# A two-layer trunk on one core: attention scores on 128 partitions, and two late FFNs that begin with plain pairs

## The chip, the cores and the metric

The kernel runs on one core of one Trainium2 chip. The metric is the device time of one execution in microseconds. Three runs of the kernel before took 2305.58, 2306.04 and 2314.34 us; the median is 2306.04 us.

## The reference

The input has 512 positions of 1024 features, in float32. Two layers, each with two half-step SwiGLU FFNs of 2816 hidden units, a mixer between them (retention in layer 0, forgetting attention in layer 1), and a gated per-layer embedding at the end. Every step is preceded by an RMS norm, and a last norm ends the trunk.

```python
for i in range(DEPTH):
    h = h + 0.5 * swiglu(rmsnorm(h, nw[0]), ffn_w_in[i, 0], ffn_w_out[i, 0])
    hn = rmsnorm(h, nw[1])
    h = h + (retention(hn, ...) if i % 2 == 0 else forgetting_attention(hn, ...))
    h = h + 0.5 * swiglu(rmsnorm(h, nw[2]), ffn_w_in[i, 1], ffn_w_out[i, 1])
    gate = sigmoid(rmsnorm(h, nw[3]) @ ple_w_gate[i])
    h = h + gate * (p[i] @ ple_w_proj[i])
return rmsnorm(h, final_norm_w)

# forgetting attention: 16 heads of 64, causal
log_f = log_sigmoid(fz + b_f)          # one gate per position and head
c = cumsum(log_f)
logits = q @ k.T * DH ** -0.5 + c[query] - c[key]
o = softmax(logits) @ v
```

## The kernel before, in words

**Numbers.** A float32 value is split into a high part that TensorE takes as it is and a low part, the rest. A product of two split values is three matmuls, high by high, high by low, low by high (`mm3`, L300 to L303). `split` (L289) makes the parts of an activation: ScalarE copies the high part, VectorE subtracts it (lines L292 and L293). Weights are loaded through `wraw` buffers, cast on ScalarE (L79), and their low part is made on VectorE or GpSimd (L80). Activations lie with features on partitions: eight blocks of 128 features by 512 positions, `h[0]` to `h[7]`.

**Norms.** The gain goes into the split; the factor per position is applied at the end of a step. `columns` (L421) adds up the squares with eight tiny matmuls (L426), and VectorE makes the reciprocal root from them (`cols`, L448 to L454). `rows` (L436) turns the result with four transposes (L445) and copies it to `rows` on ScalarE, as the factor for every product of this norm.

**FFN.** A pair is the two products, gate and up, for 128 hidden units. Most pairs take a scheme of seven instead of eight half-size products: `one` (L517), `two` (L522) and `three` (L533), all through `product` (L475, matmuls at L478), 84 matmuls of 256 columns. They need sums of weight quarters (`emit_sums`, L131) and sums of activation quarters, which `Norm.quarters` (L354) makes from each finished block of `h` on ScalarE and VectorE under names such as `t1` and `b21`. `plain` (L496) is a pair by eight products, 96 matmuls of 256 columns, with no sums. The first FFN begins with two plain pairs; the other three begin with `one` of pairs 0 and 1. Pairs are worked off in three chunks, each followed by its eight output blocks (`out_blocks`, L560).

**Retention** (L679) begins with the q and k products of head 0, then columns and rows, then v (`v_part`, L662). Its output products of the last two heads share banks (`out_both`, L634).

**Forgetting attention** (L824) has eight pairs of heads, each with its k product (`k_part`, L889), its q product (`q_part`, L906) and scores (L923). For k the low part lies in one tile `klo`, 64 partitions per head, so the matmul at L933 contracts over 64 partitions. The one at L936 contracts over 128: high and low part of q on the one side, the high part of k twice on the other. VectorE then does the softmax from the scores' banks (L955 to L967), with the gates' sums from `cdram`. `turn` (L972) transposes the probabilities, ten transposes per head at L982, into three banks, which ScalarE and VectorE split into `thi` and `tlo`. `attend` (L988) multiplies them by v (L995, L996) and adds the halves (L998 on ScalarE, L999 on VectorE). `out_part` (L620) does the output in two halves of heads, each added to `h` on its own. The gates' chain runs over 16 partitions from L836 to L868, on VectorE for the most part.

**What sets the order.** TensorE's order is the order in which the code is written. For the other engines a scheduler decides. Weights come in the order of `W.plan` (L215 to L253), two ahead of use. Eight PSUM banks rotate through one pool (`bank`, L277); a bank comes free when the last engine has read it. Which pool of activation buffers a norm takes is set at L1149 (`ua` and `ud` with 16 buffers, `ub`, `uc`).

## Time and profile before

| | |
|---|---|
| runs, median | 2306.04 us (2305.58 to 2314.34) |
| profiled execution, its own time | 2314.51 us |
| span of its profile | 2312.6 us |
| PE busy | 2192.7 us, 95% of the span, 13417 matmuls |
| DVE busy | 1537.3 us, 66% |
| ACT busy | 1210.0 us, 52% |
| POOL busy | 460.0 us, 20% |
| mean granted TensorE clock | 0.966 |

PE is TensorE's matmuls, DVE is VectorE, ACT is ScalarE, POOL is GpSimd. The profiled execution took 2314.51 us, 1.9 more than its span and 8.5 more than the median of the runs. Matmuls overlap one another, so TensorE's busy time is no measure of how densely they run: for that the starts of successive matmuls are compared. The granted clock is given as a share of full speed, 2.4 GHz; its lower level is 1.2 GHz.

### The profile page before, as it was taken

Reading aid. Unit: us, or ns where it says so; the run is one execution under the profiler, and the core shown is the slowest. Engines: PE = TensorE matmul, PEld = TensorE weight load, DVE = VectorE, ACT = ScalarE, POOL = GpSimd, SP = SyncE. Lnnn points to the kernel's source line nnn. Section 1 sums busy time; section 2 is a strip of 40 time slices with the busy share of each in tenths; the row PEclk is TensorE's granted clock in tenths of the full one; section 3 lists DMA queues with packets and bytes.
Section 4 is the critical chain, followed back from the end, with each engine's and each line's share of the span. In section 5 each row is a group of like instructions: output and inputs, shape, how many; then the busy total and the mean of one; then the engine's idle time right before and its main releaser. Section 6 shows DMA issues by size and latency. Waiting matters only on the chain.

```text
span 2312.6 us, 34447 instructions
## 1 busy us (share of the span) xinstructions
PE 2192.7 (95%) x13417; PEld 1955.9 (85%) x13417; DVE 1537.3 (66%) x2813; ACT 1210.0 (52%) x2022; POOL 460.0 (20%) x347
## 2 busy tenths in 40 slices
PE   7998999999999899999989899999999989999998
PEld 7898987888888798989879899897777779898977
DVE  8676766264453976767687676776775787676774
ACT  7464554333233673646466455455564576363653
POOL 0010103344443010101101011014222211010144
PEclk9999999999999999999999999999889989999998
DMA  6474652222322464646345465543222246464631
GB/s 192 119 179 123 150 143 93 75 96 73 100 82 73 119 163 129 156 131 157 105 127 121 130 150 152 145 115 101 65 64 82 69 108 163 117 160 132 147 109 37
DMA packets 87907, 274.94 MB, mean 119 GB/s; under 512 B 9648, under 2 KB 13232, under 8 KB 87744
## 3 DMA queue, kind: packets, MB, share of 16 engines
q1 hardware_dynamic: 63328, 209.78, 27.7%
q0 software_dynamic: 23184, 61.88, 16.0%
q8 instruction: 105, 1.72, 0.3%
q10 hardware_dynamic: 1232, 1.09, 0.1%
q14 instruction: 58, 0.48, 0.1%
HBM read 270.58 MB, written 2.13 MB: 118 GB/s over the span
## 4 chain that ended last, share of the span: by engine, by line
PE 73%; DVE 10%; ACT 7%; DMA 6%; issue 2%; POOL 0%; SPq 0%; ACTq 0%; DVEq 0%; POOLq 0%
PE bank L478 24%; PE bank L303 13%; PE bank L301 13%; PE bank L302 13%; DMA wraw<-in_ffn_w_in 5%; DVE sums L141 2%; PE bank L673 2%; PE bank L674 2%; PE bank L675 2%; ACT w L117 1%; ACT s L79 1%; DVE w L80 1%; ACT w L118 1%; PE bank L936 1%; PE bank L933 1%
## 5 line engine op out<-in xcount | busy, mean ns | idle before, releaser
L79 ACT CAST w<-wraw 128x1024 fp32r<-128x1024 f32 (+1 forms) x224 | 226.7, 1020 | 443.3 <-PE bank L303 286.4
L80 DVE TENSOR_TENSOR s<-sums,s 128x512 fp32r<-128x512 f32 x344 | 232.6, 687 | 116.0 <-ACT s L79 115.5
L79 ACT CAST s<-sums 128x512 fp32r<-128x512 f32 x344 | 208.2, 617 | 190.4 <-DVE sums L141 139.1
L303 PE MATMUL bank<-unit_a,w 128*128 128x512 f32 (+1 forms) x752 | 292.3, 389 | 4.4 <-DVE w L80 2.7
L301 PE MATMUL bank<-unit_a,w 128*128 128x512 f32 (+1 forms) x752 | 293.4, 390 | 2.4 <-ACT w L79 2.0
L302 PE MATMUL bank<-unit_a,w 128*128 128x512 f32 (+1 forms) x752 | 291.8, 388 | 0.8 <-DVE unit_a L293 0.8
L301 PE MATMUL bank<-unit_d,w 128*128 128x512 f32 (+1 forms) x744 | 287.4, 386 | 3.6 <-ACT w L79 1.8
L302 PE MATMUL bank<-unit_d,w 128*128 128x512 f32 (+1 forms) x744 | 285.6, 384 | 5.1 <-DVE unit_d L296 3.9
L303 PE MATMUL bank<-unit_d,w 128*128 128x512 f32 (+1 forms) x744 | 285.0, 383 | 2.7 <-DVE w L80 2.7
L80 POOL TENSOR_TENSOR w<-wraw,w 128x1024 fp32r<-128x1024 f32 x90 | 220.1, 2449 | 323.5 <-ACT w L79 312.5
L478 PE MATMUL bank<-unit_b,s 128*128 128x256 f32 x952 | 205.1, 282 | 0.0
L119 POOL DMA_DIRECT2D a<-in_ffn_w_in x86 | 75.2, 874 | 612.2 <-ACT a L118 540.3
L478 PE MATMUL bank<-unit_d,s 128*128 128x256 f32 x1188 | 194.3, 281 | 0.0
L119 POOL DMA_DIRECT2D w<-in_ffn_w_in x75 | 65.6, 875 | 645.2 <-ACT w L118 518.2
L478 PE MATMUL bank<-unit_a,s 128*128 128x256 f32 x1314 | 186.6, 279 | 2.9 <-ACT unit_a L361 2.4
L302 PEld LDWEIGHTS bank<-unit_d,w 128*128 128x128 f32 x744 | 145.1, 195 | 32.2 <-DVE unit_d L296 4.1
L141 DVE TENSOR_TENSOR sums<-wraw 128x512 f32<-128x512 f32 x172 | 118.0, 688 | 81.6 <-DMA wraw<-in_ffn_w_in 80.3
L301 PEld LDWEIGHTS bank<-unit_d,w 128*128 128x128 f32 x744 | 145.3, 195 | 31.5 <-ACT w L79 3.5
L478 PE MATMUL bank<-unit_b,w 128*128 128x256 f32 x774 | 147.7, 291 | 25.2 <-ACT tmp L529 24.6
L303 PEld LDWEIGHTS bank<-unit_a,w 128*128 128x128 f32 x752 | 141.5, 188 | 35.5 <-DVE w L80 4.5
L569 DVE SCALAR_TENSOR_TENSOR tmp<-bank,rows 128x512 f32<-128x512 f32 x96 | 66.0, 689 | 158.2 <-PE bank L303 154.5
L478 PEld LDWEIGHTS bank<-unit_a,s 128*128 128x128 f32 x1314 | 167.7, 190 | 3.5 <-ACT unit_a L361 2.6
(266 smaller groups left out, 4942.9 us busy)
## 6 DMA issues: line engine op xcount, KB each, us to landing
wraw<-in_ffn_w_in SPq DMA_DIRECT2D x174, 512.0 KB, 4.6
w<-in_ffn_w_in POOLq DMA_DIRECT2D x75, 512.0 KB, 5.6
wraw<-in_ffn_w_out SPq DMA_DIRECT2D x64, 512.0 KB, 5.0
a<-in_ffn_w_in POOLq DMA_DIRECT2D x86, 256.0 KB, 6.5
wraw<-in_ffn_w_out SPq DMA_DIRECT2D x32, 384.0 KB, 4.3
wraw<-in_ret_qk SPq DMA_DIRECT2D x16, 512.0 KB, 3.4
wraw<-in_ret_v SPq DMA_DIRECT2D x16, 512.0 KB, 3.7
wraw<-in_ret_g SPq DMA_DIRECT2D x16, 512.0 KB, 3.5
```

Of the source, the lines that this page charges most:

```text
L79: self.nc.scalar.copy(hi, raw)
L80: self.low.tensor_tensor(out=lo, in0=raw, in1=hi.bitcast(F32), op=ALU.subtract)
L119: self.nc.gpsimd.dma_start(out=lo, in_=src, accum_op=ALU.add)
L141: add = lambda o, p, q: nc.vector.tensor_tensor(out=o, in0=p, in1=q, op=ALU.add)
L301: nc.tensor.matmul(out, wh, xh, start=first, stop=False)
L302: nc.tensor.matmul(out, wh, xl, start=False, stop=False)
L303: nc.tensor.matmul(out, wl, xh, start=False, stop=last)
L478: add = lambda w, x, start, stop: nc.tensor.matmul(out, w, x, start=start, stop=stop, skip_group_check=True)
L569: nc.vector.scalar_tensor_tensor(out=t1, in0=o, scalar=-0.5, in1=n.r, op0=ALU.mult, op1=ALU.mult)
L673: nc.tensor.matmul(os[t], xh, wh[:, js], start=k == 0, stop=False)
L674: nc.tensor.matmul(os[t], xh, wl[:, js], start=False, stop=False)
L675: nc.tensor.matmul(os[t], xl, wh[:, js], start=False, stop=k == KB - 1)
```

## The change

Five pieces.

1. The third and fourth FFN also begin with two plain pairs, in the order low half of positions first; the columns come between the two, the rows behind `one` of the third pair. `quarters` makes `b21` earlier, and a new form `b12` for the even blocks with the last block of a norm; four more buffers of `ua` hold it (`extra`).
2. In the first FFN columns and rows move behind further products.
3. In retention the rows of the norm move behind v.
4. In the attention the k product of pair 0 goes ahead of the columns, its q product ahead of the rows. The low parts of k lie in two tiles of 128 partitions, the other half of each set to zero, so all score matmuls contract over 128 partitions. In a pair the order is now: k, q, attend 0, attend 1, turn 0, turn 1, scores.
5. In the attention's output the two halves of heads add up in the same bank (`OutBoth`), with six banks held open for the first half, and one addition to `h` per block instead of two.

```diff
-CHUNKS = ((0, 8), (8, 16), (16, 22))
-CHUNKS0 = ((0, 6), (6, 14), (14, 22))
+PLAIN = (2, 0, 2, 2)
+CHUNKS = [((0, 6), (6, 14), (14, 22)) if n else ((0, 8), (8, 16), (16, 22)) for n in PLAIN]
...
@@ Norm.quarters
+                if "b21" not in form:
+                    oh, ol = self.unit(), self.unit()
+                    part(o, oh, ol, slice(0, S))
+                    form.update(b21=(oh[:, c0], ol[:, c0]), b22=(oh[:, c1], ol[:, c1]))
+                if b == KB - 1 and self.extra:
+                    for j, x in enumerate(self.forms):
+                        u = unit(self.extra)
+                        x["b12"] = u[:, c0], u[:, c1]
+                        split(h[2 * j][:, c1], *x["b12"], self.gain[:, 2 * j : 2 * j + 1])
...
@@ plain
+            order = [(k, t) for k in range(KB) for t in range(2)]
+            if i:
+                order.sort(key=lambda kt: kt[1])
+            for k, t in order:
...
@@ ffn
-        if i == 0:
-            whole = [plain(m) for m in range(PLAIN)]
-            begun = done = PLAIN
-            n.columns()
-            start(begun)
-            one(begun)
+        if PLAIN[i]:
+            done = PLAIN[i]
+            whole = [plain(m) for m in range(done - 1)]
+            if i:
+                n.columns()
+            whole.append(plain(done - 1))
+            start(done)
+            one(done)
+            if not i:
+                n.columns()
+                two(done)
+                start(done + 1)
+                one(done + 1)
             n.rows()
             for m, (g, u) in enumerate(whole):
                 gated(m, g, u, True)
-            two(begun)
-            begun += 1
+            two(done + 1 if not i else done)
+            begun = done + (1 if i else 2)
...
@@ OutBoth
+        def first(self, ms):
+            for m in ms:
+                self.banks[m] = bank()
+                self.add(0, m)
+
+        def rest(self):
+            for m in range(KB):
+                if m not in self.banks:
+                    self.first([m])
+                self.add(1, m)
+                nc.vector.tensor_tensor(out=h[m], in0=self.banks[m], in1=h[m], op=ALU.add)
+                self.nxt.block(m)
...
@@ retention
-                    n.rows()
-                    nc.scalar.mul(epsv, spread(n.v), EPS)
...
                 vs = v_part(ret_v[hd], n)
+                if hd == 0:
+                    n.rows()
+                    nc.scalar.mul(epsv, spread(n.v), EPS)
...
@@ forgetting
             (fz,) = proj([a["fox_f"]], n)
+            begun = [proj([s], n)[0] for s in fox_qk[0][0:1]]
             n.columns()
+            begun += proj(fox_qk[0][1:2], n)
             n.rows()
...
+            lows = []
+            for e in range(2):
+                lows.append(pool.tile([P, S], F32R, name=f"klo{e}"))
+                nc.gpsimd.memset(lows[e].bitcast(F32), 0.0)
...
-                            nc.tensor.matmul(at[i], q[e][own[e], i * P : w], klo[own[e], :w], start=True, stop=False)
+                            nc.tensor.matmul(at[i], q[e][:, i * P : w], lows[e][:, :w], start=True, stop=False)
...
+            both = OutBoth([(fox_o[0], yhi, ylo), (fox_o[1], [], [])], nxt)
             for p in range(8):
+                if p < 7:
+                    k, q = k_part(p + 1), q_part(p + 1)
                 else:
+                    both.first((0, 1))
                 if old:
                     y = temp()
+                    for e in range(2):
+                        attend(p - 1, e, v, old[e], y)
                     split_y(y)
                 if p == 4:
                     v = v_block(1)
+                if p == 7:
+                    both.first((2, 3))
+                old = [turn(e, sm[e]) for e in range(2)]
+                if p < 7:
                     sm = scores(p + 1, q, k)
+            both.first((4, 5))
...
-    where = (wide_ad, ((ua, 16),), wide_ad, ((ua, 16),), wide_dd, ((ud, 16),), wide_dd, ((ud, 16),))
+    bca, bcd, bdc = ((ub, 8), (uc, 4), (ua, 16)), ((ub, 8), (uc, 4), (ud, 16)), ((ub, 8), (ud, 16), (uc, 4))
+    where = (bca, ((ua, 16),), bca, ((ua, 16),), bdc, ((ud, 16),), bcd, ((ud, 16),))
     norms = [Norm(nw(i), *where[i]) for i in range(8)] + [Norm(fw)]
+    norms[4].extra = norms[6].extra = ua
```

Three places where the order of instructions moves. Line numbers of the changed kernel differ: its `split` is at L290, its low part of q at L932, its columns and rows at L428 and L447, v at L683 to L685.

TensorE, start of retention, before: the columns (L426), the rows of two factors (L445) and the first v matmuls (L673).

```order
L303 MATMUL bank<-unit_a,w_4090 128x512
L426 MATMUL bank<-ones_r,tmp 128x2 x8
L445 MATMUL bank<-ident,cols 128x128 x4
L445 MATMUL bank<-ident,cv 128x128 x4
L673 MATMUL bank<-w_4145,unit_a 128x512
L674 MATMUL bank<-w_4145,unit_a 128x512
```

The same place in the changed kernel, the columns and what follows, and then where the rows stand:

```order
L300 MATMUL bank<-unit_a,w_4089 128x512
L428 MATMUL bank<-ones_r,tmp 128x2 x8
L683 MATMUL bank<-w_4144,unit_a 128x512
L684 MATMUL bank<-w_4144,unit_a 128x512
```

```order
L684 MATMUL bank<-w_4292,unit_a 128x512
L685 MATMUL bank<-w_4292,unit_a 128x512
L447 MATMUL bank<-ident,cols 128x128 x4
L447 MATMUL bank<-ident,cv 128x128 x4
L298 MATMUL bank<-unit_b 128x512
```

The 96 matmuls of v now stand between the columns and the rows.

VectorE, end of the first embedding, ahead of the third FFN, with the engine each row waits for, before: products times gate (L1079, L1083), addition to `h` (L1084), sums of weights (L141), their splits (L80), a form of the norm (L382).

```order
L1079 TENSOR_TENSOR tmp<-bank,rows 128x512 [waits PE_49]
L141 TENSOR_TENSOR sums<-wraw 128x512 [waits DMAHW1_49,DMAHW0_49]
L141 TENSOR_TENSOR sums<-sums,wraw 128x512 [waits DVE_49]
L1083 TENSOR_TENSOR tmp<-bank,tmp 128x512 [waits PE_49,Activation_49]
L1084 TENSOR_TENSOR hall<-hall,tmp 128x512 [waits DVE_49]
L80 TENSOR_TENSOR s_11441<-sums,s_11441 128x512 [waits Activation_49]
L141 TENSOR_TENSOR sums<-sums,wraw 128x512 [waits DVE_49]
L382 SCALAR_TENSOR_TENSOR tmp<-tmp 128x256 [waits Activation_49]
```

The changed kernel, from the third-last block on (L1088, L1092 and L1093 are the product, its gate and the addition, L293 the split of a `b12`, `hall` is `h`):

```order
L1088 TENSOR_TENSOR tmp<-bank,rows 128x512
L414 TENSOR_TENSOR acc<-acc,tmp 128x512 [waits Activation_49]
L359 TENSOR_TENSOR unit_d<-tmp,unit_d 128x256 [waits Activation_49]
L1092 TENSOR_TENSOR tmp<-bank,tmp 128x512 [waits Activation_49]
L293 SCALAR_TENSOR_TENSOR unit_a<-hall,small,unit_a 128x256 [waits PE_49]
L1093 TENSOR_TENSOR hall<-hall,tmp 128x512 [waits DVE_49]
L293 SCALAR_TENSOR_TENSOR unit_a<-hall,small,unit_a 128x256 [waits PE_49]
L293 SCALAR_TENSOR_TENSOR unit_a<-hall,small,unit_a 128x256 [waits Activation_49]
L388 SCALAR_TENSOR_TENSOR tmp<-tmp 128x256 [waits Activation_49]
L393 TENSOR_TENSOR tmp<-tmp 128x256
```

The splits of `b12` stand between the additions of the embedding, and the first two wait for TensorE; the sums of weights no longer stand there.

VectorE, one attention pair, before: q's factor (L910), its low parts (L917), an attend's addition (L999), splits of a turn (`tlo`), of y (`unit_a`), and the first step of the softmax (L955).

```order
L910 SCALAR_TENSOR_TENSOR tmp<-bank,rows 128x512
L917 TENSOR_TENSOR q_16257<-tmp,q_16257 64x512
L917 TENSOR_TENSOR q_16260<-tmp,q_16260 64x512
L999 TENSOR_TENSOR tmp<-bank,tmp 64x512
L293 TENSOR_TENSOR tlo_16280<-bank,thi_16279 128x512 x2
L293 TENSOR_TENSOR unit_a<-tmp,unit_a 128x512
L293 TENSOR_TENSOR tlo_16280<-bank,thi_16279 128x256
L955 ISA p_16329,sm_16328<-bank,unit_c 128x128
```

The changed kernel, the same steps (q L925 and L932, attends L1014, splits L290, softmax L970):

```order
L925 SCALAR_TENSOR_TENSOR tmp<-bank,rows 128x512
L932 TENSOR_TENSOR q_15955<-tmp,q_15955 64x512
L932 TENSOR_TENSOR q_15958<-tmp,q_15958 64x512
L1014 TENSOR_TENSOR tmp<-bank,tmp 64x512 x2
L290 TENSOR_TENSOR tlo_15991<-bank,thi_15990 128x512 x2
L290 TENSOR_TENSOR unit_a<-tmp,unit_a 128x512
L290 TENSOR_TENSOR tlo_15991<-bank,thi_15990 128x256
L290 TENSOR_TENSOR tlo_16012<-bank,thi_16011 128x512 x2
L290 TENSOR_TENSOR tlo_16012<-bank,thi_16011 128x256
L970 ISA p_16061,sm_16060<-bank,unit_c 128x128
```

Both attends' additions and all the splits of both turns now stand between q's low parts and the softmax; before, those of one turn stood ahead of q.

## Rows read from the trace of the kernel before

**Rows 1.** TensorE's waits, whole span; columns: us in total, times, longest us.

```profile
PE bank L445 <- DVE cols L454: 18.5, 4, 7.1
PE bank L478 <- ACT unit_d L369: 16.4, 2, 9.0
PE bank L936 <- DVE q L917: 7.6, 6, 1.3
```

**Rows 2.** Busy time by window: us, PE, PEld, DVE, ACT, POOL busy, PEclk, DMA, GB/s.

```profile
385.00:420.00 35.00, 26.14 (x112) 21.33 (x111) 16.61 (x22) 10.19 (x13) 12.13 (x5) 0.85 0.19 61
1199.60:1235.00 35.40, 23.75 (x161) 22.87 (x161) 29.49 (x59) 23.82 (x42) 3.49 (x4) 0.81 0.51 127
1570.70:1611.10 40.40, 37.07 (x158) 30.12 (x156) 24.19 (x38) 19.68 (x29) 14.22 (x9) 0.92 0.27 91
1638.30:1809.60 171.30, 164.26 (x698) 128.01 (x697) 118.49 (x402) 95.46 (x207) 46.75 (x28) 0.87 0.21 67
1663.70:1689.40 25.70, 24.29 (x101) 18.79 (x101) 18.69 (x64) 14.27 (x32) 6.18 (x4) 0.83 0.20 62
1863.50:1895.00 31.50, 20.86 (x143) 20.28 (x142) 25.88 (x54) 22.28 (x38) 2.62 (x3) 0.77 0.55 130
```

**Rows 3.** The chain of waits, between 990 and 1020 us; columns: start us, us, what.

```profile
1002.16 9.94 PE bank L478 x84
```

**Rows 4.** Timeline of PE, first rows of retention; columns: start us, us, instruction, [idle].

```profile
399.15 0.39 PE L301 MATMUL bank<-unit_a,w 128*128 128x512 f32 x1
...
399.83 0.95 PE L426 MATMUL bank<-ones_r,tmp 128*128 128x2 f32 x8
407.93 1.12 PE L445 MATMUL bank<-ident,cols 128*128 128x128 f32 x4 [7.15 <-DVE cols L454]
```

**Rows 5.** Timeline of DVE, last addition of the first embedding, ahead of the third FFN.

```profile
1213.64 0.69 DVE L1084 TENSOR_TENSOR hall<-hall,tmp 128x512 f32<-128x512 f32 x1
```

**Rows 6.** Timeline of DVE, first and last step of the forget gates' chain.

```profile
1577.37 0.68 DVE L836 TENSOR_TENSOR tmp<-bank,rows 16x512 f32<-16x512 f32 x1 [1.83 <-ACT rows L439]
...
1601.19 0.66 DVE L868 TENSOR_TENSOR tmp<-tmp,spans 16x496 f32<-16x496 f32 x1
```

**Rows 7.** Timeline of PE, one pair: turn, projection, attend, turn.

```profile
1766.52 1.28 PE L982 MATMUL bank<-ident,p 128*128 128x128 f32 x10
1767.56 0.47 PE L301 MATMUL bank<-unit_d,w 128*128 128x512 f32 x1
...
1773.12 0.40 PE L995 MATMUL bank<-thi,unit_b 128*128 128x512 f32 x1
...
1774.34 1.28 PE L982 MATMUL bank<-ident,p 128*128 128x128 f32 x10
```

**Rows 8.** Timeline of PE, the first scores, and the projection behind them.

```profile
1611.11 0.61 PE L933 MATMUL bank<-klo,q 64*128 64x256 f32 x2
1611.66 0.61 PE L936 MATMUL bank<-khi,q 128*128 128x256 f32 x2
...
1615.71 0.40 PE L301 MATMUL bank<-unit_d,w 128*128 128x512 f32 x1
```

**Rows 9.** Timeline of DVE, one attention pair.

```profile
1654.43 0.68 DVE L910 SCALAR_TENSOR_TENSOR tmp<-bank,rows 128x512 f32<-128x512 f32 x1
1655.80 2.60 DVE L917 TENSOR_TENSOR q<-tmp,q 64x512 fp32r<-64x512 f32 x2 [0.69 <-ACT q L916]
...
1659.15 1.29 DVE L293 TENSOR_TENSOR tlo<-bank,thi 128x512 fp32r<-128x512 f32 x2
...
1661.29 0.28 DVE L955 CUSTOM_DVE_ANT_0 p<-bank,unit_c 128x128 f32<-128x128 f32 x1
...
1667.52 0.15 DVE L964 TENSOR_SCALAR sm<-sm 128x1 f32<-128x1 f32 x1
1671.94 0.69 DVE L893 TENSOR_TENSOR tmp<-bank,rows 128x512 f32<-128x512 f32 x1 [4.28 <-PE bank L303]
...
1677.98 0.69 DVE L900 TENSOR_TENSOR klo<-tmp,khi 64x512 fp32r<-64x512 f32 x1
```

127 lines of the change are left out of this document (42 added, 85 removed).

## Prediction

> **What bounds the kernel now.** I read the list of TensorE's waits first, then windows laid around the stages that the change touches, then timelines inside these. TensorE sets the time, so the question is where it stands still and where it runs slowly. Three kinds of wait lie in the touched places [rows 1]: 18.5 us for the four `cols` chains (columns, then rows, of a norm), 16.4 us for the first products of the third and fourth FFN (two waits, 9.0 and 7.4 us), and 7.6 us for `q` inside the attention's scores. The windows show the second cost [rows 2]: around each wait the granted clock is low, 0.77 to 0.85 of full speed where a stage begins and 0.83 in an attention pair.
>
> To see what a stage loses, I compare its length with what it holds at the dense rate: a 256-wide matmul starts every 118.3 ns (84 in 9.94 us) [rows 3], a 512-wide one every 0.227 us (three in 0.68 us) [rows 4].
> - Retention's start, 35.0 us: 96 wide matmuls (21.8 us) and 16 small ones (about 1.8) make 23.6, so 11.4 are lost, 7.15 of them in one wait [rows 2, 4].
> - Third FFN's start, 35.4 us: 161 at 118.3 ns make 19.0; 16.4 lost, 9.0 in one wait [rows 1, 2].
> - Fourth FFN's start, 31.5 us: 143 make 16.9; 14.6 lost, 7.4 in one wait [rows 1, 2].
> - Forgetting attention's start, 40.4 us: 158 PE instructions, 12 of them small, make 34.4; 6.0 lost [rows 2].
> - The six attention pairs, 171.3 us, 25.7 in the one shown [rows 2].
>
> **The change part by part.**
>
> *Retention* moves the rows behind v's 96 matmuls, 21.8 us of cover for a chain that TensorE now waits 7.15 us for [rows 4]. The wait goes, and with it most of the slow stretch behind it (11.4 - 7.15 = 4.3 in clock and a late weight; I take 2.3 of it, since the weight is as late as before). The next thing late is that weight. **-9.5 us**, between -7.1 (the wait alone) and -11.4 (all).
>
> *Third FFN.* Two pairs by eight products hold 96 instead of 84 matmuls each: 24 x 118.3 ns = +2.84 us [rows 3]. What they buy is that they need only the plain quarters and no sums of weights. Now the last addition of the embedding before it ends on DVE at 1214.33, 14.7 us behind TensorE's last matmul at 1199.6 [rows 2, 5]. The new DVE order puts the four extra `b12` splits into this queue, and the first of them waits for TensorE to release a unit. Behind it stand 26 rows up to the last addition. At 0.69 us for a full row [rows 5] and 0.42 for a half one they take some 16 us; begun when the last gate products read their operands, about 6 to 8 us before the end, they put the addition 7.5 to 9.7 us behind it. Two casts and two splits follow (2.2 us). The first plain pair runs 42 matmuls, 5.0 us, before it needs them. So a wait of 4.7 to 6.9 us stays; I take 5.8, the middle. The second weight of the first pair reuses a buffer that the pair itself holds: 1.8 us more, estimated as load to cast. With 1.9 us of slow clock the new loss is 5.8 + 1.8 + 1.9 + 2.84 = 12.3 against 16.4: **-4 us**, between +2 (wait as now, plus the products) and -10 (no wait).
>
> *Fourth FFN.* The additions in front of it shrink from two per output block to one, and the last two blocks come 24 matmuls apart, so DVE is level when they end. I expect no wait in the first pair, 0.8 us for the weight, +2.84: 14.6 - 3.6 = **-11 us**, between -6 (half of the 7.4 stays, with its clock) and -13.
>
> *First FFN.* Columns and rows move behind products of the next pair. One of the four waits on `cols` is here, but the products put in its place need weights that come about as late as the rows did. **0**, -4 to +4. The chunks of FFNs three and four shift by two pairs with the same work: **0**, +-5.
>
> *Attention's start.* k's projection goes ahead of the columns, q's ahead of the rows, so the `cols` wait is covered (most of the 6.0). But the gate chain starts behind q's projection: 48 wide matmuls, 10.9 us, later in the order. It runs from 1577.37 to past 1601.19 [rows 6], some 24 us, and has to be back before the first softmax, with v's 21.8 us beside it. The softmax is a few us late, half hidden by the next pair's projections. **-3 us**, +4 to -12.
>
> *The six attention pairs.* TensorE's work in a pair, at full clock: two projections of 24 matmuls, 5.56 us each, two attends of 1.22, two turns of 1.04 [rows 7], and scores. The scores now take 4.60 us even at full clock with no stall (1611.11 to 1615.71) [rows 8]. On 128 partitions they are 16 matmuls with the widths of two attends, 2.44 us. So 11.1 + 2.4 + 2.1 + 2.4 = 18.1 us.
>
> A row tells why: a pair of 64-row products takes 0.61 us, its 128-row partner 0.61 too, and the first begins 0.55 us before the second [rows 8], so 64 rows save nothing. The section's 4.60 us are 2.16 more than the dense 2.44, which I put down to the changes between the two shapes; all of it goes. The Trainium skill, TensorEngine Tiling (Array Packing), Overview, speaks against the change: with a contraction of 64 or less the array can be split into independent tiles, for a speedup up to 2x. By that rule an estimated 5 us would be given up and 2267 come out (rival G); by the rows nothing is, and the sum goes by them.
>
> But DVE then sets the pair. Its chain: softmax of both heads 6.2 us (1661.29 to 1667.52); k's product to the second low part 6.7 (1671.94 to 1678.67); q's product and its low parts 4.0 (1654.43 to 1658.40); two attend additions and seven split pieces at about 0.65 each (1.29 for two), 5.0 [rows 9]. Together 21.9. The order changes too: all splits of the turns now stand directly ahead of the softmax, and the scores behind the turns need the banks these splits release. TensorE therefore waits 2 to 4 us per pair ahead of the scores, where now it waits at most 1.3 [rows 1], and the clock falls behind such a wait, as it does now. I take 22.5 us: the DVE chain and 0.6 for clock. Five pairs at 22.5 and one with v's half (18.1 + 21.8 + 2.7 = 42.6) make 155.1: **-16 us** of 171.3. The ends are 0 (waits and clock eat it all) and -27 (18.1 and 1 us in each, v's pair without loss).
>
> *Output of the attention.* Same matmuls, eight fewer DVE additions, held banks: 0.
>
> The sum: -9.5 - 4 - 11 + 0 - 3 - 16 = **-43.5 us**. It is made against the profiled execution, 2314.51 us (span 2312.6 and 1.9 around it), which is 8.5 us, 0.4%, above the median of the runs, 2306.04; the difference carries over, so 2306.0 - 43.5 = **2262.5 us**.
>
> **The rivals.**
> - *B, the scores' wait eats the pairs.* Waits of 2 to 4 us bring the half clock in each pair; k's projection then ends later, and DVE's chain starts from it: period 24.5 to 25.5. For it: six of eight score sections wait for `q` and 0.83 is granted in such a pair. Against it: DVE stands idle 4.3 us ahead of k's product now [rows 9], so it has room. Loop -2 instead of -16: **2276**.
> - *C, the third FFN and the attention's start bring nothing*: `b12` splits hold DVE up further, and the gate chain is late in full. +2 and +4 instead of -4 and -3; with half of the loop's gain, **2284**.
> - *E, all covered.* No clock loss in the pairs (20 us each, v's pair 41, so -30), -10 in the third FFN: **2242**.
> - *D, slower: the half clock for whole pairs.* If the wait ahead of the scores comes in every pair and the granted clock stays at 1.2 GHz until the next one, the 18.1 us become 36, plus a wait of 2: 38 against 25.7, +12 x 6 = +74, and with the other -27 **2353**. It turns the sum positive when a pair passes 25.7 + 27/6 = 30.2 us, that is with 10 or more of its 18.1 us of work at half clock; the slow share of the pair shown is about 0.17 x 2 of 25.7, 8.7 us at half clock for 4.4 of work.
> - *G, the narrow products are cheap now.* If two 64-row products ran side by side, the low half of the dense 2.44 us, 1.22, would be worth only 0.61, and widening would cost 0.61 in each of eight sections, 5 us: **2267**. Against it stand the equal 0.61 us of both shapes [rows 8]. The Trainium skill's page named above states this as a speedup up to 2x; the trace disagrees.
> - *F, it doesn't do what it says*: scores still wait for their low parts and the plain pairs for their quarters; each place trades one wait for another. **2303**.
>
> **How the numbers follow.** Forecast (2250 to 2270) 0.42, G 0.02, B 0.26, E 0.13, C 0.09, F 0.05, D 0.03. The range reaches to E and C: **2240 to 2289**. Half a percent is 11.5 us, about what a measurement of this kernel tells from no change: faster than 2294.5 takes the forecast, G, B, E and nearly all of C, 0.91; F and the rest of C make 0.06 the same; D 0.03 slower.
>
> **What would show it.** Right: `cols` is gone from retention's and both late FFNs' waits; the 64-row shape is gone from the scores, whose section lasts near 2.5 to 3.5 us; a pair lasts 22 to 23 us, with DVE busy in nearly all of it and TensorE waiting on a bank or a split ahead of the scores; the third FFN still waits 5 to 6 us for a `b21` or `b22` operand. Wrong: a pair over 24 us, or a clock below 0.8 in pairs; a wait for the softmax over 5 us in the first pair; a wait for weights in the plain pairs over 3 us.

## The result, and the profile after

The changed kernel takes 2285.89 us, median of four runs (2275.98 to 2291.95), against 2308.25 for the kernel before in the runs beside it: a ratio of 0.9895, 95% interval 0.9854 to 0.9937. That is 22.4 us, or 1%, faster, half of the 43.5 us forecast. The forecast was 2262.5 us and faster; the range, 2240 to 2289, holds the time, near its upper end. The profiled execution took 2285.92 us, its span is 2284.1.

A stage below runs from the start of its first matmul in the trace to that of the next stage, the rest to the start of the last matmul. Both columns are from the one profiled execution of each kernel; between executions a stage that no edit touches still differs by some 4 us (the second FFN took 348.3 to 352.7 us in the profiled executions of all kernels here). The sum of -27.5 us is larger than the 22.4 of the medians because the profiled execution of the kernel before, 2314.51 us, lies 6.3 above its median, that of the changed kernel on it.

| stage | before | changed | difference | forecast |
|---|---|---|---|---|
| first FFN | 370.4 | 370.5 | +0.2 | 0 |
| retention, to the end of rows and v | 57.1 | 47.4 | -9.7 | -9.5 |
| rest of retention | 360.0 | 358.3 | -1.7 | 0 |
| second FFN, first embedding | 406.6 | 407.2 | +0.7 | 0 |
| third FFN | 365.8 | 374.3 | **+8.5** | **-4** |
| attention, to the end of the second scores | 72.8 | 69.0 | -3.7 | -3 |
| six attention pairs | 171.3 | 156.6 | -14.7 | -16 |
| last pair and output | 54.0 | 53.2 | -0.8 | 0 |
| fourth FFN | 365.8 | 360.8 | **-5.1** | **-11** |
| rest | 74.9 | 73.9 | -1.0 | 0 |
| sum | 2298.6 | 2271.1 | -27.5 | -43.5 |

The list of TensorE's waits in the changed kernel, whole span (us in total, times, longest):

```profile
PE bank L480 <- ACT tmp L532: 29.6, 18, 2.8
PE bank L480 <- DMA w<-in_ffn_w_in: 14.4, 4, 4.6
PE bank L948 <- DVE tmp L1014: 9.0, 10, 1.5
...
PE bank L511 <- DVE w L79: 4.0, 4, 1.9
PE bank L447 <- DVE cols L456: 3.6, 1, 3.6
...
PE bank L300 <- POOL w L79: 1.7, 1, 1.7
```

Against [rows 1], `cols` (now line L447) has fallen from 18.5 us to 3.6, and the two waits of 16.4 us for a form of the norm at the products are gone from the list. In their place stand 14.4 us for a DMA into `w`, and several kinds at L511, the plain pairs. The wait for `q` in the scores has become one for the addition of an attend (L1014).

Windows of the changed kernel, columns as in [rows 2]: retention's start; the third FFN, its two plain pairs and what follows; the six pairs, one of them, and the one with v's half; the fourth FFN, plain pairs and what follows.

```profile
375.00:422.00 47.00, 45.29 (x203) 37.12 (x202) 21.32 (x27) 14.97 (x19) 22.19 (x10) 1.00 0.28 88
1189.10:1229.00 39.90, 31.03 (x210) 29.64 (x209) 26.84 (x49) 19.71 (x34) 1.76 (x2) 0.83 0.33 93
1231.10:1280.00 48.90, 42.84 (x351) 42.43 (x350) 34.05 (x60) 31.04 (x54) 5.25 (x6) 0.93 0.57 140
1632.40:1788.90 156.50, 143.91 (x697) 119.80 (x696) 125.78 (x411) 95.48 (x210) 46.92 (x28) 0.95 0.24 75
1655.00:1676.90 21.90, 19.55 (x102) 16.24 (x101) 19.53 (x62) 14.71 (x33) 6.20 (x4) 0.98 0.26 73
1699.50:1742.30 42.80, 41.38 (x198) 34.15 (x197) 22.90 (x70) 21.97 (x45) 15.74 (x8) 0.99 0.26 87
1842.10:1868.00 25.90, 25.20 (x210) 25.00 (x209) 21.84 (x41) 15.64 (x26) 1.77 (x2) 1.00 0.49 142
1870.10:1918.00 47.90, 42.34 (x351) 41.93 (x350) 34.06 (x60) 31.12 (x54) 5.45 (x7) 0.96 0.59 142
```

Retention's start runs at full clock (0.85 in [rows 2]); the one wait left there is 1.7 us for the low part of a weight (L300). The two plain pairs of the third FFN, 192 products of 118.3 ns or 22.7 us, with the columns and some ten products of the third pair take 39.9 us at a clock of 0.83. In the fourth the same work takes 25.9 us at full clock. But behind them both FFNs lose again: the 348 products of the window from 1231.1 are worth 41.2 us and take 48.9, those from 1870.1 take 47.9. The timeline of PE (start us, us, instruction, idle before it and its releaser) shows what stands there, third FFN first:

```profile
1197.45 0.38 PE L511 MATMUL bank<-unit_d,w 128*128 128x256 f32 x1 [3.15 <-ACT unit_d L366]
...
1202.45 0.58 PE L511 MATMUL bank<-unit_c,w 128*128 128x256 f32 x1 [2.54 <-ACT unit_c L358]
...
1215.56 3.14 PE L511 MATMUL bank<-unit_b,w 128*128 128x256 f32 x13 [1.89 <-DVE w L79]
...
1238.33 0.80 PE L480 MATMUL bank<-unit_b,w 128*128 128x256 f32 x2 [4.56 <-DMA w<-in_ffn_w_in]
```

```profile
1855.95 1.82 PE L511 MATMUL bank<-unit_b,w 128*128 128x256 f32 x13 [0.70 <-DVE w L79]
...
1876.92 0.50 PE L480 MATMUL bank<-unit_b,w 128*128 128x256 f32 x2 [4.18 <-DMA w<-in_ffn_w_in]
```

3.15 and 2.54 us are waits for the last quarters, 1.89 for the low part of the second pair's second weight, which takes a buffer that the first pair holds until it ends. The prediction had these sizes, though it put the weight's wait into the first pair, where only 0.49 us stand. It did not have the last one, 4.56 us in the third FFN and 4.18 in the fourth: the weight of the second seven-product pair. The timelines of ACT and POOL, third FFN:

```profile
1227.85 1.05 ACT L116 CAST w<-wraw 128x1024 fp32r<-128x1024 f32 x1 [11.45 <-PE bank L511]
1228.80 1.06 ACT L117 ACTIVATE w<-wraw 128x1024 fp32r<-128x1024 f32 x1
```

```profile
1230.15 0.88 POOL L118 DMA_DIRECT2D w<-in_ffn_w_in  x1 [18.90 <-ACT w L117]
```

ScalarE stood idle for 11.45 us until the second plain pair released a weight's buffer at 1227.85. Then come a cast, a negation, and a DMA that adds the weight into the low part; the product that reads it starts at 1238.33, 10.5 us after the release. TensorE had 44 products in hand: 36 of the third pair and eight of this one, which read only the weight's high part.

### The profile page after: what moved, and what is told of

Same layout as the page of the kernel before. It is cut to its first block, busy times and chain, and to the rows that moved or that the text cites. A ratio compares the mean times of both kernels' runs of the same rounds, so it can differ in the third digit from the quotient of the medians.

```text
span 2284.1 us, 34483 instructions
## 1 busy us (share of the span) xinstructions
PE 2170.2 (95%) x13465; PEld 1950.0 (85%) x13465; DVE 1530.0 (67%) x2775; ACT 1195.3 (52%) x1993; POOL 453.6 (20%) x339
## 4 chain that ended last, share of the span: by engine, by line
PE 76%; DVE 11%; ACT 5%; DMA 4%; issue 3%; POOL 1%; SPq 0%; ACTq 0%; DVEq 0%; POOLq 0%
PE bank L480 29%; PE bank L300 13%; PE bank L298 13%; PE bank L299 13%; DMA wraw<-in_ffn_w_in 3%; PE bank L511 2%; PE bank L683 2%; PE bank L684 2%; PE bank L685 2%; DVE sums L140 1%; DVE w L79 1%; DMA w<-in_ffn_w_in 1%; ACT w L116 1%; ACT w L117 1%; ACT s L78 1%
## 5 line engine op out<-in xcount | busy, mean ns | idle before, releaser
L78 ACT CAST w<-wraw 128x1024 fp32r<-128x1024 f32 (+1 forms) x233 | 236.0, 1021 | 428.4 <-PE bank L300 275.0
L79 DVE TENSOR_TENSOR s<-sums,s 128x512 fp32r<-128x512 f32 x328 | 221.9, 686 | 133.6 <-ACT s L78 133.0
L78 ACT CAST s<-sums 128x512 fp32r<-128x512 f32 x328 | 199.0, 617 | 183.8 <-DVE sums L140 116.0
L300 PE MATMUL bank<-unit_a,w 128*128 128x512 f32 x736 | 287.0, 390 | 4.3 <-DVE w L79 2.6
L298 PE MATMUL bank<-unit_a,w 128*128 128x512 f32 x736 | 287.9, 391 | 1.6 <-ACT w L78 1.6
L299 PE MATMUL bank<-unit_a,w 128*128 128x512 f32 x736 | 286.6, 389 | 0.2 <-DVE unit_a L290 0.2
L298 PE MATMUL bank<-unit_d,w 128*128 128x512 f32 (+1 forms) x728 | 276.4, 380 | 3.5 <-ACT w L78 1.8
L299 PE MATMUL bank<-unit_d,w 128*128 128x512 f32 (+1 forms) x728 | 275.3, 378 | 4.0 <-DVE unit_d L293 2.9
L300 PE MATMUL bank<-unit_d,w 128*128 128x512 f32 (+1 forms) x728 | 274.6, 377 | 2.7 <-DVE w L79 2.7
L480 PE MATMUL bank<-unit_b,s 128*128 128x256 f32 x904 | 193.1, 280 | 0.0
L480 PE MATMUL bank<-unit_d,s 128*128 128x256 f32 x1140 | 181.8, 280 | 0.0
L79 DVE TENSOR_TENSOR w<-wraw,w 128x1024 fp32r<-128x1024 f32 (+1 forms) x144 | 168.5, 1176 | 18.7 <-ACT w L78 18.4
L480 PE MATMUL bank<-unit_b,w 128*128 128x256 f32 x738 | 139.5, 289 | 37.2 <-ACT tmp L532 22.8
L300 PEld LDWEIGHTS bank<-unit_a,w 128*128 128x128 f32 x736 | 138.1, 188 | 35.3 <-DVE w L79 4.3
L298 PEld LDWEIGHTS bank<-unit_d,w 128*128 128x128 f32 x728 | 139.7, 192 | 30.9 <-ACT w L78 3.4
L298 PEld LDWEIGHTS bank<-unit_a,w 128*128 128x128 f32 x736 | 138.3, 188 | 31.9 <-ACT w L78 3.5
```

Source lines behind the costliest of these rows:

```text
L78: self.nc.scalar.copy(hi, raw)
L79: self.low.tensor_tensor(out=lo, in0=raw, in1=hi.bitcast(F32), op=ALU.subtract)
L298: nc.tensor.matmul(out, wh, xh, start=first, stop=False)
L299: nc.tensor.matmul(out, wh, xl, start=False, stop=False)
L300: nc.tensor.matmul(out, wl, xh, start=False, stop=last)
L480: add = lambda w, x, start, stop: nc.tensor.matmul(out, w, x, start=start, stop=stop, skip_group_check=True)
```

## The experiments

Each is an edit of the changed kernel. Stage lengths are from the one profiled execution of each.

**The third FFN by seven products again.**

```diff
-PLAIN = (2, 0, 2, 2)
+PLAIN = (2, 0, 0, 2)
```

> The changed kernel, but the third FFN begins with `one` of two pairs as before (7 products). Theory: in the changed kernel the plain start of the third FFN costs more than it brings (stage 379.7 us against 371.3 before). The stage goes back to 371 to 372 us and the time falls by some 8 us, to about 2277. Rival 1, the loss comes from elsewhere in the stage (its chunks, the weights' order, the embedding's results in other buffers): the stage stays at 377 or more. Rival 2, the stage gains but the embedding before it or the attention behind it pays: stage 371, time unchanged.

2276.35 us (ratio to before 0.987, 0.9838 to 0.9902, which overlaps the changed kernel's 0.9854 to 0.9937). The third FFN's stage fell from 374.3 to 360.6 us, more than expected; both rivals fall, since no other stage grew. (The lengths in the text above, 379.7 and 371.3, count the attention's first projection in, some 5.4 us.) The wait for the form of the norm that the plain pairs were to spare is back in full, and still the stage is 13.7 us shorter. Over all runs it took 372.4 us on average with plain pairs as in the change (four executions, 367.8 to 377.5) and 360.9 with seven products (eight, 358.5 to 363.4). The kernel before took 365.8 in its one, with the same wait. Its excess lies behind the rows: up to the first output blocks the same 594 products took 76.7 us there, with two waits for a copy (2.84 and 0.68 us), and 68.2 in each of the eight executions (the chunk behind it was 1 to 5 us shorter there). Which of the other edits took these 8.5 us away no run shows. The windows, the kernel before first:

```profile
1231.30:1308.00 76.70, 70.85 (x594) 70.06 (x593) 55.26 (x100) 49.23 (x85) 10.47 (x12) 0.98 0.67 164
1218.40:1286.60 68.20, 68.20 (x594) 68.20 (x593) 56.00 (x101) 51.33 (x88) 10.50 (x12) 1.00 0.76 188
```

Timeline of PE, start of the third FFN by seven products, to be read against the four waits above:

```profile
1195.96 0.58 PE L480 MATMUL bank<-unit_d,w 128*128 128x256 f32 x1 [9.22 <-ACT unit_d L366]
...
1211.05 0.51 PE L480 MATMUL bank<-unit_b,w 128*128 128x256 f32 x2 [3.22 <-ACT tmp L532]
```

**The low part of that weight on VectorE.**

```diff
-        for m in [PLAIN[i]] + [k1 + 1 for _, k1 in chunks[:-1]]:
+        for m in [PLAIN[i]] + ([PLAIN[i] + 1] if PLAIN[i] else []) + [k1 + 1 for _, k1 in chunks[:-1]]:
```

> The changed kernel, but the low part of the second seven-product pair's first weight is made on VectorE and not by an accumulating DMA, in the three FFNs that begin plain. Theory: TensorE waits 4.6 us (third FFN), 4.2 us (fourth) and 2.8 us (first) for these transfers, since the weight's buffer comes free only when a plain pair ends. Without the transfer the third and fourth stages shorten by 5 to 7 us each (wait and the slow clock behind it), the time by 10 to 14 us. Rival: the cast ahead of it is late too, and the wait on a DMA turns into one on ACT or DVE for the same weight: each stage shortens by under 2 us.

2270.61 us (0.9848, 0.9824 to 0.9871). The third stage took 366.5 us, 7.8 less than in the changed kernel and 5.9 less than the average just given; the fourth took 354.8, 5.9 less. No wait for a DMA is left in the two late FFNs; the next one at that place is 1.77 us for a copy at L532. Between the rows and the first output block, where the edit acts, the third FFN took 44.4 us against 49.2 to 49.5 in the four executions with the transfer, the fourth 44.3 against 47.2 to 49.3 in five. In these two FFNs the rival falls. In the first the edit brought nothing: the wait of 2.81 us for the transfer went, but the one for `cols` behind it grew from 3.55 us to 7.28, and the first output block came no sooner (89.9 us against 88.7):

```profile
50.88 1.08 PE L447 MATMUL bank<-ident,cols 128*128 128x128 f32 x4 [7.28 <-DVE cols L456]
```

**Low products on 64 partitions again.**

```diff
-nc.tensor.matmul(at[i], q[e][:, i * P : w], lows[e][:, :w], start=True, stop=False)
+nc.tensor.matmul(at[i], q[e][own[e], i * P : w], lows[e][own[e], :w], start=True, stop=False)
```

> The changed kernel, but the low products of the scores contract over 64 partitions as before. Theory: narrow products save nothing; a score section lasts 4.6 us at the least against a dense 2.4, the softmax starts about 1.2 us later and the six pairs last 164 to 168 us against 156.6. Rival G: narrow products are cheaper, and the six pairs last the same or up to 4 us less.

The six pairs took 179.0 us (the one execution 2294.93), 22.5 more: twice the theory, and rival G is off by its sign. The order of a pair is the changed one, and TensorE waits for the same things nearly as long, but the window shows a clock of 0.85 where the changed kernel has 0.95. The second line is one of its slow stretches:

```profile
1624.70:1803.70 179.00, 168.70 (x697) 130.44 (x696) 126.13 (x413) 95.70 (x212) 46.78 (x28) 0.85 0.21 65
1645.80:1655.80 10.00, 10.00 (x23) 6.77 (x23) 9.02 (x48) 3.73 (x13) 0.64 (x1) 0.50 0.11 26
```

The timeline of PE, the scores of one pair and the projection behind them:

```profile
1643.80 0.38 PE L948 MATMUL bank<-klo,q 64*128 64x256 f32 x1 [1.49 <-DVE tmp L1014]
1644.52 0.49 PE L948 MATMUL bank<-klo,q 64*128 64x512 f32 x1 [0.33 <-DVE tmp L1014]
...
1646.76 0.69 PE L951 MATMUL bank<-khi,q 128*128 128x384 f32 x1
...
1651.16 0.63 PE L298 MATMUL bank<-unit_d,w 128*128 128x512 f32 x1
...
1652.44 0.63 PE L298 MATMUL bank<-unit_d,w 128*128 128x512 f32 x1
...
1656.13 0.39 PE L298 MATMUL bank<-unit_d,w 128*128 128x512 f32 x1
...
1656.83 0.39 PE L298 MATMUL bank<-unit_d,w 128*128 128x512 f32 x1
```

And two such places in the changed kernel, and the longest slow stretch in its six pairs:

```profile
1649.60 0.38 PE L948 MATMUL bank<-klo,q 128*128 128x256 f32 x1 [1.46 <-DVE tmp L1014]
...
1654.87 0.63 PE L298 MATMUL bank<-unit_d,w 128*128 128x512 f32 x1
...
1655.97 0.40 PE L298 MATMUL bank<-unit_d,w 128*128 128x512 f32 x1
...
1672.52 0.39 PE L948 MATMUL bank<-klo,q 128*128 128x256 f32 x1 [1.47 <-DVE tmp L1014]
1673.23 0.50 PE L948 MATMUL bank<-klo,q 128*128 128x512 f32 x1 [0.33 <-DVE tmp L1014]
...
1676.59 0.34 PE L951 MATMUL bank<-khi,q 128*128 128x384 f32 x1
```

```profile
1761.50:1768.30 6.80, 6.44 (x19) 5.16 (x18) 6.68 (x36) 3.19 (x12) 0.00 (x0) 0.50 0.10 37
```

The waits ahead of the sections are the same, 1.49 and 0.33 us against 1.47 and 0.33. With 64-row products behind them, a 384-wide matmul takes 0.69 instead of 0.34 us three microseconds later, and the projection runs at half rate until 1656: three of its matmuls take 1.28 us at first, 0.70 later. The granted clock falls to 0.50 behind all six sections of these pairs, for 6.8 to 10.3 us. With 128 rows everywhere it does not always stay up: it falls behind four of the six (at 1649.60 the projection starts at half rate too, at 1672.52 it does not), but for 3.4 to 6.9 us.

**The old order of a pair, scores on 128 partitions.**

```diff
                 if p < 7:
-                    k, q = k_part(p + 1), q_part(p + 1)
+                    k = k_part(p + 1)
...
                 if old:
                     y = temp()
-                    for e in range(2):
-                        attend(p - 1, e, v, old[e], y)
+                    attend(p - 1, 0, v, old[0], y)
+                    new = [turn(0, sm[0])]
+                if p < 7:
+                    q = q_part(p + 1)
+                if old:
+                    attend(p - 1, 1, v, old[1], y)
                     split_y(y)
...
-                old = [turn(e, sm[e]) for e in range(2)]
+                new.append(turn(1, sm[1]))
+                old = new
```

> The changed kernel, but a pair's order is as before (k, attend 0, turn 0, q, attend 1, turn 1, scores), with the scores on 128 partitions. Theory: both parts matter; TensorE waits for q's low part again, 1.3 us and the slow clock behind it, and a pair lasts about 23.5 to 24.5 us: six pairs 163 to 168 us. Rival: the order is worth nothing and the widening all: six pairs 155 to 158 us. Other rival: the order is worth all: 170 us.

The six pairs took 146.3 us, less than every theory allowed. Against the kernel before, whose order these pairs have, that is the widening: 25.0 us. Against the changed kernel it is the order alone, which costs 10.3 us. The one execution took 2273.29 us. Waits of TensorE in these pairs, and the window:

```profile
PE bank L948 <- DVE q L932: 10.6, 5, 2.2
```

```profile
1632.00:1778.30 146.30, 134.95 (x698) 114.51 (x697) 117.58 (x405) 97.05 (x210) 47.44 (x28) 0.99 0.25 80
```

TensorE waits for q's low part as it did before, even longer (2.2 us against 1.3 in [rows 1]), and the clock is 0.99, against 0.87 in [rows 2]: it falls behind one of the six sections, for 3.4 us. In the kernel before it fell behind all five that had a wait of 1.3 us, for 6.9 to 10.3. Narrow products alone don't bring it down, since the sections of that kernel without a wait kept it [rows 8]. A wait ahead of wide products brings it down sometimes, behind one of six sections here and four of six in the changed kernel, a wait ahead of narrow ones every time.

**A third order: k, q, attend 0, turn 0, attend 1, turn 1, scores.**

```diff
                 if p < 7:
                     k, q = k_part(p + 1), q_part(p + 1)
...
                 if old:
                     y = temp()
-                    for e in range(2):
-                        attend(p - 1, e, v, old[e], y)
+                    attend(p - 1, 0, v, old[0], y)
+                new.append(turn(0, sm[0]))
+                if old:
+                    attend(p - 1, 1, v, old[1], y)
                     split_y(y)
...
-                old = [turn(e, sm[e]) for e in range(2)]
+                new.append(turn(1, sm[1]))
+                old = new
```

> The changed kernel, but a pair's order is k, q, attend 0, turn 0, attend 1, turn 1, scores: both projections ahead, as the change has it, and the turns between the attends, as before. With the old order the six pairs lasted 146.3 us, with the changed one 156.6. Theory: what costs 10 us is that the scores' first banks are those of both attends, which VectorE empties only behind q's low parts; with a turn between the attends the first banks come free earlier, and q's product has 4.2 us of cover: six pairs 140 to 148 us. Rival: what costs is that k and q come together and VectorE idles ahead of k and then has both on its chain: six pairs 153 to 158 us.

146.5 us (the one execution 2259.11), as the theory had it; the rival falls. The projections may stand together; what costs 10 us is the two attends side by side. The waits for the attends' additions (9.0 us, ten times, in the changed kernel) are 6.1 us, five times, and the clock is 0.99 instead of 0.95; the shorter waits alone would not make 10 us. The waits and the window:

```profile
PE bank L948 <- DVE tmp L1014: 6.1, 5, 1.5
```

```profile
1621.10:1767.60 146.50, 138.14 (x697) 114.89 (x697) 121.43 (x410) 97.06 (x210) 46.76 (x28) 0.99 0.26 80
```

**Both late FFNs by seven products.**

```diff
-PLAIN = (2, 0, 2, 2)
+PLAIN = (2, 0, 0, 0)
```

> The changed kernel, but the third and the fourth FFN both begin by seven products. Theory: plain is a loss in the third FFN (13.7 us against the changed kernel) and a gain in the fourth, where it left no wait for a form of the norm. The third stage is 360 to 366 us, the fourth goes back up from 355 to 361 to some 364 to 367, and the time is 2278 to 2283. Rival: the fourth FFN's start loses as well once the weights' waits are counted; the stage falls to 352 to 355 and the time to 2270 or less.

2267.52 us (0.9831, 0.9817 to 0.9846). The third stage took 359.2 us, the fourth 353.8 against 360.8: the rival holds, and the plain beginning gains nothing in the fourth FFN either. How much it loses is less certain. Over all runs this stage took 358.0 us on average with plain pairs as in the change (five executions, 354.6 to 360.8), 355.2 with the low part on VectorE (four, 352.8 to 358.5), and 355.5 with seven products (three, 353.8 to 356.4): 2.5 us less than plain, with ranges that overlap. With seven products there is a wait for a form of the norm; timeline of PE, start of the fourth FFN, and its rows:

```profile
1835.23 1.08 PE L480 MATMUL bank<-unit_d,w 128*128 128x256 f32 x2 [6.88 <-ACT unit_d L366]
...
1851.96 0.60 PE L447 MATMUL bank<-ident,cols 128*128 128x128 f32 x4
```

**Both by seven, and two additions per output block.**

```diff
-PLAIN = (2, 0, 2, 2)
+PLAIN = (2, 0, 0, 0)
...
-    W.plan += fox_o[0][0:3] + fox_o[1][0:3] + [fox_o[0][3], fox_o[1][3]]
+    W.plan += fox_o[0] + fox_o[1]
...
-                    both.first((0, 1))
+                    out_part(fox_o[0], yhi[0:4], ylo[0:4], None, range(1))
...
-                    both.first((2, 3))
+                    out_part(fox_o[0], yhi[0:4], ylo[0:4], None, range(1, 2))
...
-            both.first((4, 5))
+            out_part(fox_o[0], yhi[0:4], ylo[0:4], None, range(2, 4))
...
-        both.rest()
+        out_part(fox_o[1], yhi[4:8], ylo[4:8], nxt)
```

> Both late FFNs by seven products, and the attention's output in two halves with two additions per block, as before; the pairs' order is the changed one. With one addition per block the fourth FFN began by seven products without any wait for a form of the norm, and its stage lasted 353.8 us (365.8 before). Theory: it is the halved additions, not the plain pairs, that took the 7.4 us wait away. With two additions the wait for the last block's form is back, 6 to 9 us, and the stage lasts 362 to 367 us. Rival: the earlier b21 split and the other pools took it away; no such wait, and the stage lasts 352 to 356 us.

The premise of this text, that no wait for a form was left with one addition, was a misreading: the 6.88 us above are that wait. The stage took 361.4 us in its one execution (the one execution of the kernel 2274.00), just short of the theory and far from the rival; that is 7.6 more than the run just told and 5.9 more than its average. The waits are:

```profile
1837.08 1.04 PE L480 MATMUL bank<-unit_d,w 128*128 128x256 f32 x2 [7.65 <-ACT unit_d L366]
...
1858.09 0.65 PE L447 MATMUL bank<-ident,cols 128*128 128x128 f32 x4 [3.08 <-DVE cols L456]
```

Halving the additions shortens the wait for the form only from 7.65 to 6.88 us, but it removes the one of 3.08 us for `cols`. From the FFN's first product to its rows it is 24.5 us with one addition (1827.48 to 1851.96) and 29.5 with two (1828.55 to 1858.09). The rest of the difference comes later and is within what executions differ by.

**Versions put together.** First the third FFN by seven products, the old order of a pair (edit above), and in the fourth FFN plain pairs with the low part on VectorE:

```diff
-PLAIN = (2, 0, 2, 2)
+PLAIN = (2, 0, 0, 2)
...
-        for m in [PLAIN[i]] + [k1 + 1 for _, k1 in chunks[:-1]]:
+        for m in [PLAIN[i]] + ([3] if i == 3 else []) + [k1 + 1 for _, k1 in chunks[:-1]]:
```

> The changed kernel with the third FFN by seven products, the old order in a pair (scores on 128 partitions), and in the fourth FFN the second pair's low part made on VectorE. Theory: the parts add up: the pairs 146 us (10 less than the changed kernel), the third FFN 361 to 366 (8 to 14 less), the fourth 353 to 357 (0 to 5 less): 2256 to 2267. Rival: what is gained in the attention and the third FFN's end shifts waits to the next stage, and the sum is half: 2270 or more.

2253.71 us (0.9773, 0.9757 to 0.9789): the parts add up. The pairs took 146.3 us, the third FFN 363.4, the fourth 352.8. Then the old order with seven products in both late FFNs, `PLAIN = (2, 0, 0, 0)`:

> Both late FFNs by seven products, the old order in a pair, everything else as changed. Theory: plain pairs bring nothing in the fourth FFN once the additions are halved, so this is within 3 us of the version with a plain fourth FFN and a low part on VectorE, 2253.7: 2251 to 2257, with the fourth stage 352 to 356. Rival: with the shorter attention the fourth FFN's start waits again without plain pairs: stage 358 or more, time 2258 or more.

2256.14 us (0.9779, 0.9754 to 0.9805), the fourth stage 356.4. The time is the theory's; the wait is there again (6.92 us), as the rival has it, and yet the stage is as long as the average above. The same with the weights' low parts on VectorE during the attention:

```diff
             cdram = dram.tile([FH, S], F32, name="cdram")
-            W.low = nc.gpsimd
+            W.low = nc.vector
```

> The same, but the low parts of the weights in the attention are made on VectorE and not on GpSimd. In the pairs the two low parts of q take 2.55 us where the second low part of k takes 0.69 alone, and a split of a weight runs on GpSimd for 2.35 us at that time. Theory: the two get in each other's way, q's low part comes 1 to 1.9 us earlier, and the wait of 2.1 us ahead of the scores shrinks by as much: six pairs 136 to 142 us against 146.3. Rival: two more VectorE operations of 1.2 us per pair are on its chain and eat this: 146 us or more.

2252.72 us (0.9772, 0.9746 to 0.9797). The pairs took 144.1 us, 2.1 less, half of the least that the theory gave. The mechanism is there, its worth small. Timelines of VectorE and GpSimd in a pair, old order and low parts on GpSimd:

```profile
1647.83 2.60 DVE L932 TENSOR_TENSOR q<-tmp,q 64x512 fp32r<-64x512 f32 x2 [0.69 <-ACT q L931]
```

```profile
1646.81 2.35 POOL L79 TENSOR_TENSOR w<-wraw,w 128x1024 fp32r<-128x1024 f32 x1 [4.83 <-ACT w L78]
```

And VectorE with the low parts on VectorE:

```profile
1652.13 1.22 DVE L79 TENSOR_TENSOR w<-wraw,w 128x1024 fp32r<-128x1024 f32 x1
1653.38 1.41 DVE L932 TENSOR_TENSOR q<-tmp,q 64x512 fp32r<-64x512 f32 x2
```

The two low parts of q take 1.41 instead of 2.60 us, but the weight's own 1.22 us now stand ahead of them. At last the first version of this group with the weights' low parts on VectorE, and the same in the third order of a pair:

> Third FFN by seven products, the old order in a pair, the weights' low parts in the attention on VectorE, and a plain beginning of the fourth FFN whose second pair has its low part made on VectorE. With seven products there too, this took 2252.7. Theory: in the fourth FFN a plain beginning without the transfer is worth 2 to 4 us (it has no wait of 6.9 us, but 2.8 us more of products): 2247 to 2253. Rival: it is worth nothing: 2253 to 2257.

> The same, but the order k, q, attend 0, turn 0, attend 1, turn 1, scores in a pair. That order waits on the attend's addition instead of q's low part; both of these stand behind q's low parts on VectorE. Theory: the pairs are bounded by VectorE's chain either way: six pairs 143 to 146 us, as in the old order, and the time within 3 us of the other. Rival: with 4.2 us of cover for q the faster low part takes the wait away altogether: six pairs 132 to 140 us.

2253.26 us (0.9756, 0.9731 to 0.978) and 2251.53 (0.9749, 0.9724 to 0.9774); pairs 143.8 and 143.3 us, fourth FFN 354.8 and 358.5. By its time the first run sides with its rival, that the plain beginning is worth nothing there even without the transfer (2252.72 with seven products). By the ratios to the kernel before, 0.9756 against 0.9772 with overlapping intervals, it may gain a few us; that stays open. In the second the pairs are the theory's. These two and the three before them lie within 5 us of each other; all are 2.2 to 2.5% faster than the kernel before, and better than the change.

## Why the prediction was right or wrong

**Right.** Retention came out at -9.7 against -9.5: the wait went, full clock, and the weight's late arrival stayed (1.7 us). The attention's start gave -3.7 against -3, the first half as reasoned: 6.2 us less up to the first scores. Behind them it took 2.4 more, with TensorE waiting for VectorE's splits of v (3.0 us) and for q (2.5). In the changed kernel the pair with v's half took 42.8 us against 42.6, the five others 22.8 on average (156.6 less 42.8, by five) against 22.5, the one shown 21.9; VectorE was busy for 19.5 of the 21.9 us, and TensorE waited for a bank ahead of the scores, as forecast. VectorE's rows in that pair:

```profile
1653.96 0.28 DVE L970 CUSTOM_DVE_ANT_0 p<-bank,unit_c 128x128 f32<-128x128 f32 x1
...
1660.94 0.69 DVE L909 TENSOR_TENSOR tmp<-bank,rows 128x512 f32<-128x512 f32 x1
...
1668.75 3.00 DVE L932 TENSOR_TENSOR q<-tmp,q 64x512 fp32r<-64x512 f32 x2 [0.74 <-ACT q L931]
...
1676.88 0.28 DVE L970 CUSTOM_DVE_ANT_0 p<-bank,unit_c 128x128 f32<-128x128 f32 x1
```

The chain from k's product to the next softmax is 15.9 us here (1660.94 to 1676.88), and the softmax ahead of it makes up the rest, 7.0 us from 1653.96. It was forecast as 15.7 and 6.2. A score section lasts 3.6 to 5.3 us, waits included, not the 2.5 to 3.5 named as a sign.

**The step that failed: "Third FFN", -4 us.** It came out at +8.5. The term had the quarters' wait right (5.8 forecast; 3.15 + 0.64 + 2.54 + 0.15 = 6.5 measured) and the size of a second weight's (1.8; 1.89, one pair later than it said). It had the slow clock too small: 1.9 us forecast, where 39.9 us at a clock of 0.83 lose 6.8. What it lacked is the weight of the *next* seven-product pair. Two plain pairs occupy four weights where two seven-product pairs occupy two, the pool has three buffers, and so this weight could not even be cast until the second plain pair ended. The run with its low part on VectorE prices that at 6 to 8 us of the stage in the third FFN and at 3 to 6 in the fourth; in the stretch between the rows and the first output block, which differs less between executions, at 5 and at 3 to 5. The prediction followed the reuse of buffers for one weight and stopped; its own sign of being wrong, a wait for weights of over 3 us, stood one pair further on. The other part is the plain beginning itself: with 6.5 and 1.89 us of waits, the slow clock and 2.84 of products, it still costs 5.6 us more than seven products with their 9.22 (366.5 in one execution against 360.9 on average).

The same hole is in "Fourth FFN", -11 us, which came out at -5.1. There the other half of the reasoning failed as well. With the additions halved, seven products lose less there than the kernel before did, and the plain start, which waits for 0.70 us where seven products wait for 6.88, gives all of that back: 2.84 us for 24 more products, 4.18 at the DMA and the slow clock behind it. What the stage gained does not come from the plain pairs. The halved additions, which the prediction entered as 0 under "Output of the attention" and named only as the reason why VectorE would be level, are worth 5.9 to 7.6 us by the run with two. That run, without plain pairs and without halved additions, took 361.4 us, 4.4 less than the kernel before; as in the third FFN, no run shows which of the other edits that belongs to.

**Right in sum, wrong in its parts: "The six attention pairs", -16 us.** The measured -14.7 is 25.0 gained by the widening and 10.3 lost by the order; that they nearly make the forecast is luck. The prediction gave the widening 2.16 us per section, from a section at full clock, and let the half clock behind the sections hang on the wait alone. It hangs on the shape of the products too, and the widening takes most of it away: in the old order the clock is 0.99 with wide products, after longer waits, against 0.87 with narrow ones [rows 2], in the changed order 0.95 against 0.85. And the prediction took VectorE's chain of 21.9 us for what sets a pair. In the order that the change makes the pair shown lasts as long, with VectorE busy for 19.5 us of it; but in the old order the same operations go into 20.7 us a pair, so the chain is no floor, and the prediction did not ask what the old order would make of wide scores.

The rule of the Trainium skill, TensorEngine Tiling (Array Packing), Overview, by which a contraction of 64 can be up to twice as fast, is not borne out here: in this use, without two tiles at once, narrow products cost 22.5 us over six pairs, the clock that they bring down included. Rival G falls with it. Rival B's waits did come (9.0 us for L1014), its half clock only in part (0.95, with pairs of 21.9 to 24.2 us where it had 24.5 to 25.5); D's clock never came. C's place was the third FFN, for another reason than it gave.

The first FFN's 0 is measured as +0.2. It hides two movements: to its first output block it takes 5.2 us longer, with the same kind of wait on a DMA, and gains 5.0 in the two chunks behind. Why the chunks gain I did not try.

## What to carry to other kernels

When a step is put in front to cover a wait, follow the buffers that it holds to the first step behind it: here 44 products had to cover a chain of 10.5 us that starts only at the release. A gain that was summed from one stage should be priced part by part, since two parts of one change can have opposite signs, and here the version that undoes the worse parts is twice as good as the change. And where a clock falls behind a wait, look at the shape of the work behind it, too, before blaming the wait alone.

## What the runs showed of the hardware

Behind score sections with matmuls on 64 rows beside ones on 128, the granted clock fell to 1.2 GHz (0.50) for 6.8 to 10.3 us in all six pairs of one order, with waits of 1.49 and 0.33 us in or ahead of most sections, and behind the five with a wait in the other; without a wait it kept near 2.4 GHz [rows 8]. With the same matmuls on 128 rows it fell behind four of six after the same waits, for 3.4 to 6.9 us, and behind one of six after waits of 2.1 to 2.2 us, for 3.4. So 128 rows make such falls fewer and shorter, and do not rule them out: behind waits of 3.15 and 2.54 us in the third FFN, all on 128 rows, the clock was 0.83. Why the 64-row matmuls weigh so much no run shows. The dense 16 matmuls of a section then take 2.75 us (1649.85 to 1652.60 in the old order) where the mixed ones took 4.60 in [rows 8] at full clock.

Two VectorE subtractions that read two operands from SBUF took 2.60 us together while a GpSimd subtraction was running, from 1646.81 to 1649.16, and 1.41 without it. They ended 1.27 us behind GpSimd's end, close to the 1.41 that they take alone. The Trainium skill, SBUF — State Buffer, section "SBUF: two separate sides", says that such a VectorE operation and a GpSimd operation exclude each other on a shared pair of ports for a whole instruction; these rows agree.
